# First feed-forward of a two-layer backbone: tiles 2 and 3 of the gated products by seven quarter products in place of eight

## The chip, the cores and the metric

One core of one Trainium2 chip runs the whole program. The metric is the device time in microseconds (us) of one execution, as the median of several runs. A profile is one further execution, with its own time.

## The reference, cut to what matters

Two layers work on 512 latent tokens and 256 context tokens of width 1024. Layer 0 is windowed attention, layer 1 is retention; each is followed by a gated feed-forward. The change touches the feed-forward of layer 0, where latent and context tokens go through the same weights:

```python
def swiglu(h, w_in, w_out):
    gate, up = jnp.split(h @ w_in, 2, axis=-1)
    return (jax.nn.silu(gate) * up) @ w_out

x = x + mx[5] * swiglu(modulate(rms_norm(x, norm2_g[i]), mx[3], mx[4]), ffn_w_in[i], ffn_w_out[i])
y_ctx = y_ctx + mc[5] * swiglu(modulate(rms_norm(y_ctx, norm2_g[i]), mc[3], mc[4]), ffn_w_in[i], ffn_w_out[i])
```

The inner width is 2816, or 22 tiles of 128. Beside this, all 48 modulation columns of layer 1 (`c_act @ ada_w[1] + ada_b[1]`, 6 parts of 8 columns) are worked out during this stage.

## The kernel before, in words

Everything is float32 in the reference; the kernel splits each operand of a product into a high part and a low rest (a cast on ACT, a subtraction on DVE: `split`, L157, lines L165 and L166; or `next_w`, L132, lines L140 and L141) and adds three matmuls (high by high, low by high, high by low; `mm3` at L148 to L150, `product` at L829 with its matmul at L835).

**The stage.** The hidden operand of the first feed-forward is held transposed, eight contraction pieces `A[k, half]` by two halves of 384 tokens (the 768 tokens of both streams together). The 22 inner tiles are counted by `f` from 0 and grouped 2, 4, 4, 4, 4, 4. For each tile the gate and the up product are made, then silu and the product of both, which is split into `act`. After the first tile of a group, `output` (L1007) multiplies the tiles of the group before by the second weight and adds into the residuals with `gated_add` (L253). Below, "output 0" is that of tiles 0 and 1, "output 1" that of tiles 2 to 5, and so on.

**Two ways for a tile.** `plain` (L922) makes four products of 384 columns (gate and up by two halves), each with eight contraction pieces: 8 quarter products of 12 matmuls, 96 in all. `seven` (L954) makes the same 2 by 2 block product by seven quarter products, 84 matmuls. For that it needs sums of weight quarters, four subtractions on DVE of 512 columns (L960, L962, L963, L966), then three split pairs of 1024 columns (`b11`, `b24`, `b3`) and one of 512 (`t1`, tiles `bhi` and `blo`), and on the side of the tokens the sums `S[1]` to `S[4]`. `token_sums` (L882) makes `S[1]` to `S[3]` and parks the fourth difference in the tile `crow` (L890); `last_sum` (L895) splits that into `S[4]`. After the products, seven DVE operations of 384 columns put the tile together (L977, L985, L987, and L908 and L166 twice). The seven products run in this order: 11 by `b11`, 12 by `b11`, `S[2]` by `b24`, `S[1]` by `t1`, `S[3]` by `b3`, `S[4]` by `b3`, 22 by `b24`.

Tiles 0 and 1 are made in `first_two` (L930) beside the shaping of the context half. Before, tiles 2 and 3 are plain and tiles 4 to 21 go by seven (`PLAIN = 4`).

**Buffers.** Raw weights come by SP's queue into `wraw`: two buffers in `rp`, one in `fp` (`raw_turn`, L943, one in three). Split weights have two buffers in `rp` and one in `fp`, taken in turns of three by `w_parts` (L122 and after). The operand tiles `aq` have 20 buffers: eight for `A[k, 1]`, and twelve into which the weights of two modulation units of layer 0 are loaded (units 10 and 11, L1036 to L1043); `S[1]` to `S[3]` take these twelve when the units' matmuls have read them, and `S[4]` takes those of `A[0, 1]` to `A[3, 1]`, when the last plain tile has read them. A unit ends by a transposition and two small additions (`ends`, L308 to L318); its rows wait in one of the two buffers `sq`.

**The modulation of layer 1.** `cond_rows` (L255) loads the broadcast conditioning rows into `crow` by SP's queue and applies silu; from then on `ada_next` (L947) is called at fixed places of the program: in each `seven` (behind its last split of weights), after each `seven` but the first of a group (after tile 6 all the same), and four times in each `output` but the last. Each call takes the next column from a list of 48: POOL's queue loads 512 KB into the only buffer `adaw` (L268), and DVE reduces it against the rows (L271), twice for the first 16 columns (both streams), once for the other 32, which use the free half of `crow` as a second buffer in turns.

**What sets the order.** In this stage no order is written out by hand. The instructions are put in order for each engine when the program is built, by a planner that takes program order as priority and a model of durations; on the chip each engine runs its list in that order, so an instruction that waits holds back all behind it on its engine.

Of the kernel before, what the change touches and what calls it, by code (L numbers as in the profile page):

```python
# [49 lines left out]
def dit_kernel(ctx, tc, xT, cT, crow, small, consts, masks, tabs0, tabs1, jtab, adaQ, adaN, adaT, wst, out):  # L50
# [11 lines left out]
    def T(pool, cols, tag, bufs, dt=F32):  # L62
        return pool.tile([P, cols], dt, tag=tag, bufs=bufs, name=tag)
# [42 lines left out]
    def silu(out_, in_):  # L106
        ins = nc.scalar.activation(out_, in_, AF.Silu)
        after(ins, turn["silu"][:1] or turn["lnexp"])
        turn["silu"].append(ins)
# [10 lines left out]
    def w_raw(pool=None, bufs=2):  # L120
        raw = T(pool or rp, 1024, "wraw", bufs)
        nc.sync.dma_start(raw, wst[wpos[0]])  # L122
        wpos[0] += 1
        return raw

    def w_parts(pool, own=2):

        bufs = own
        if ring:
            pool, bufs = ring[wsel[0] % len(ring)], 2  # L130
        elif wsel[0] % (2 + own) < 2:
            pool, bufs = rp, 2  # L132
        wsel[0] += 1
        return T(pool, 1024, "whi", bufs, F32R), T(pool, 1024, "wlo", bufs, F32R)

    def next_w(pool, own=2, raw=None):

        raw = raw or w_raw()
        hi, lo = w_parts(pool, own)
        nc.scalar.copy(hi, raw)  # L140
        nc.vector.tensor_tensor(lo, raw, hi, op=sub)  # L141
        return hi, lo
# [112 lines left out]
    def cond_rows(pool):  # L255

        cr = T(pool, 2048, "crow", 1)
        nc.sync.dma_start(cr, crow.broadcast_to([P, 2048]))
        for i in range(2):
            silu(cr[:, i * 1024:(i + 1) * 1024], cr[:, i * 1024:(i + 1) * 1024])  # L260
        return cr
# [537 lines left out]
    cres = load_stream(1)  # L799
    At.close()  # L800
    AK.close()
    PLAIN = 4
    WIDE = SX + SC
    THIRDS = (slice(0, 384), slice(384, WIDE))
    E = ExitStack()
# [46 lines left out]
    fp = F.enter_context(tc.tile_pool(name="fp", bufs=1, reuse_waits="tile"))  # L852
# [42 lines left out]
    def last_sum():  # L895
        for k in range(4):
            S[4, k] = parts(quarter())
            split(park[:, k * 384:(k + 1) * 384], *S[4, k])
# [5 lines left out]
    def new_act():  # L904
        return T(ep, 2 * WIDE, "act", 5, F32R)

    def finish_half(a, i, t, up):
        nc.vector.tensor_tensor(t, t, up, op=mult)  # L908
        c = THIRDS[i]
        return split(t, a[:, c], a[:, c.start + WIDE:c.stop + WIDE])  # L910

    def project_half(w, i, tag):
        o = bank(tag)
        project(w, [A[k, i] for k in range(KT)], o)
        return o

    def gate_half(w, i):
        t = t_hn(384)
        silu(t, project_half(w, i, "X"))
        return t  # L920

    def plain(w, ts=()):  # L922

        a = new_act()
        ts = [*ts, *(gate_half(w[0], i) for i in range(len(ts), 2))]
        for i in range(2):
            finish_half(a, i, ts[i], project_half(w[1], i, "Y"))
        return a

    def first_two(w, w1):  # L930

        a, ts = new_act(), []
        for i in range(2):
            X, Y = bank("X"), bank("Y")
            project_pair(w, [A[k, i] for k in range(KT)], (X, Y), None if i else context_shape)
            t = t_sq(384)
            silu(t, X)
            finish_half(a, i, t, Y)
            if i == 0:
                ts.append(gate_half(w1[0], 0))  # L940
        return a, plain(w1, ts)

    def raw_turn():  # L943
        raws[0] += 1
        return w_raw(None if raws[0] % 3 else fp, 2 if raws[0] % 3 else 1)

    def ada_next(behind):  # L947

        if ada_q:

            w = cr[:, 1024:2048] if len(ada_q) < 32 and len(ada_q) % 2 else None
            ada_tile(*ada_q.pop(0), cr, [behind], fp, w)

    def seven():  # L954
        g, u = raw_turn(), raw_turn()
        l_, r_ = slice(0, 512), slice(512, 1024)
        b11 = w_parts(fp, 1)
        split(g, *b11)
        t1 = T(fp, 512, "bhi", 1, F32R), T(fp, 512, "blo", 1, F32R)
        nc.vector.tensor_tensor(g[:, l_], u[:, l_], g[:, l_], op=sub)  # L960
        split(g[:, l_], *t1)
        nc.vector.tensor_tensor(g[:, l_], u[:, r_], g[:, l_], op=sub)  # L962
        nc.vector.tensor_tensor(g[:, r_], g[:, r_], g[:, l_], op=sub)  # L963
        b24 = w_parts(fp, 1)
        half = split(g, *b24)
        nc.vector.tensor_tensor(u[:, l_], u[:, r_], u[:, l_], op=sub)  # L966
        b3 = w_parts(fp, 1)
        split(u, *b3)
        if cr:
            ada_next(half)  # L970
        X, Y, Z = bank("X"), bank("Y"), bank("Z")
        c11, c12, c22, c21 = t_hn(384), t_hn(384), t_sq(384), t_sq(384)
        a = new_act()
        product(Y, operand["11"], b11, 0, True)
        nc.scalar.copy(c11, Y)  # L975
        product(X, operand["12"], b11, 512, True)
        nc.vector.tensor_tensor(c11, c11, X, op=add)  # L977
        silu(c11, c11)
        product(Y, operand[2], b24, 0, False)
        nc.scalar.copy(c12, Y)  # L980
        product(Z, operand[1], t1, 0, True)
        nc.scalar.copy(c21, Z)
        product(Y, operand[3], b3, 0, False)
        nc.scalar.copy(c22, Y)
        nc.vector.tensor_tensor(c22, c22, c21, op=add)  # L985
        product(Z, operand[4], b3, 512, False)
        nc.vector.tensor_tensor(c12, c12, Z, op=add)  # L987
        finish_half(a, 0, c11, c12)
        product(Y, operand["22"], b24, 512, False)
        silu(c21, Y)  # L990
        return a, finish_half(a, 1, c21, c22)
# [9 lines left out]
    def spare_w():  # L1001

        raw, w = w_raw(), (T(fp, 1024, "wraw", 1, F32R), T(fp, 1024, "adaw", 1, F32R))
        split(raw, *w)
        return w
# [30 lines left out]
    def unit(u):  # L1036
        w = [T(hq, 768, "aq", 20)[:, 0:512] for _ in range(KT - 4 * (u == 11))]
        if u == 11:
            more = T(fp, 2048, "crow", 1)
            w += [more[:, i * 512:(i + 1) * 512] for i in range(4)]  # L1040
        for k in range(KT):
            nc.sync.dma_start(w[k], adaN[u, k // 2][:, k % 2 * 512:k % 2 * 512 + 512])
        return ada_unit(u, w, pj, columns)  # L1043
# [7 lines left out]
    first = first_two([next_w(fp, 1), next_w(fp, 1)], [next_w(fp, 1), spare_w()])  # L1051
    columns = cond_columns(hq)
    ends = [unit(10), unit(11)]
    token_sums()
    f, prev = 0, None
    for gsz in FFN_GROUPS:
        acts = []
        for i in range(gsz):
            if f < PLAIN:
                acts.append(first[f] if f < 2 else plain([next_w(fp, 1, raw_turn()) for _ in range(2)]))  # L1060
                if f in (1, 2):
                    ends.pop(0)()
            else:
                if f == PLAIN:
                    last_sum()
                a, end = seven()
                acts.append(a)
                if f == PLAIN:
                    cr = cond_rows(fp)
                if i or f == PLAIN + 2:  # L1070
                    ada_next(end)
            if i == 0 and prev is not None:
                output(prev, False)
            f += 1
        prev = acts
# [464 lines left out]
    fp = F.enter_context(tc.tile_pool(name="fp", bufs=1, reuse_waits="tile"))  # L1540
# [87 lines left out]
    first = first_two()  # L1628
    f, prev = 0, None
    for gsz in FFN_GROUPS:  # L1630
        acts = []
# [158 lines left out]
```

## Time and profile before

| | us |
|---|---|
| median of 3 runs (lowest, highest) | 1782.94 (1782.34, 1787.02) |
| the profiled execution's own time | 1781.98 |
| its span in the trace | 1780.2 |
| matmuls on PE, share of the span | 97% |
| DVE, share of the span | 76% |

The profiled execution took 1.78 us more than its span, and 0.96 us less than the median of the runs. The span is cut by engine: PE is TensorE's matmuls, PEld its weight loads, DVE the vector engine, ACT the scalar engine, POOL the general engine, SP the queue that issues most transfers. A matmul's record (about 335 ns for 384 columns) is longer than its distance to the next one, since matmuls overlap; a stage is therefore measured from the start of its first matmul to the start of the next stage's. The stages around the change, by those starts in the trace:

| stage | from | to | us |
|---|---|---|---|
| tile 2, plain | 423.73 | 440.46 | 16.73 |
| output 0 | 440.46 | 457.37 | 16.91 |
| tile 3, plain | 457.37 | 474.02 | 16.65 |
| tiles 4, 5, 6, by seven | 474.02 | 517.72 | 43.70 |
| output 1 | 517.72 | 551.17 | 33.45 |
| tiles 7 to 10, by seven | 551.17 | 613.26 | 62.09 |

### The profile page before, as it was taken

Reading aid. Unit: us, or ns where it says so; the run is one execution under the profiler, and the core shown is the slowest. Engines: PE = TensorE matmul, PEld = TensorE weight load, DVE = VectorE, ACT = ScalarE, POOL = GpSimd, SP = SyncE. Lnnn points to the kernel's source line nnn. Section 1 sums busy time; section 2 is a strip of 40 time slices with the busy share of each in tenths; the row PEclk is TensorE's granted clock in tenths of the full one; section 3 lists DMA queues with packets and bytes.
Section 4 is the critical chain, followed back from the end, with each engine's and each line's share of the span. In section 5 each row is a group of like instructions: output and inputs, shape, how many; then the busy total and the mean of one; then the engine's idle time right before and its main releaser. Section 6 shows DMA issues by size and latency. Waiting matters only on the chain.

```text
span 1780.2 us, 27618 instructions
## 1 busy us (share of the span) xinstructions
PE 1721.0 (97%) x10876; PEld 1530.2 (86%) x10876; DVE 1346.5 (76%) x2347; ACT 834.1 (47%) x1465; POOL 134.4 (8%) x275
## 2 busy tenths in 40 slices
PE   6999999999999999999998999999999999999999
PEld 4777776789999999999977788898897899999998
DVE  6697786786688877787789858758758798777774
ACT  5476676454333424242455534534524564445442
POOL 0035334000000000000010000000000000000000
PEclk9999999999999999999999999999999999999999
DMA  9510002534153434353332534434433323333222
GB/s 342 229 36 25 25 1 84 161 108 139 67 154 119 154 119 153 107 157 104 119 130 86 167 107 131 148 103 137 150 104 119 95 72 111 98 112 107 95 84 83
DMA packets 59890, 206.68 MB, mean 116 GB/s; under 512 B 6640, under 2 KB 7024, under 8 KB 59504
## 3 DMA queue, kind: packets, MB, share of 16 engines
q1 hardware_dynamic: 52848, 179.75, 31.3%
q0 software_dynamic: 6912, 25.17, 4.6%
q8 instruction: 85, 1.39, 0.3%
q14 instruction: 45, 0.37, 0.1%
HBM read 202.80 MB, written 2.10 MB: 115 GB/s over the span
## 4 chain that ended last, share of the span: by engine, by line
PE 72%; DVE 15%; DMA 5%; ACT 3%; issue 2%; POOL 2%; SPq 0%; DVEq 0%; ACTq 0%; POOLq 0%
PE Y L835 13%; PE Z L835 6%; PE pj L148 6%; PE pj L150 6%; PE pj L149 6%; DMA wraw<-in_wst_dram 3%; PE X L835 3%; PE Z L1192 3%; PE Y L1179 3%; DVE wlo L166 3%; PE pT L707 2%; PE S L684 2%; PE pO L719 2%; PE X L1179 1%; POOL pr L698 1%
## 5 line engine op out<-in xcount | busy, mean ns | idle before, releaser
L165 ACT CAST whi<-wraw 128x1024 fp32r<-128x1024 f32 x171 | 179.1, 1051 | 289.9 <-PE Z L150 73.6
L166 DVE TENSOR_TENSOR wlo<-wraw,whi 128x1024 fp32r<-128x1024 f32 x171 | 208.7, 1223 | 45.4 <-ACT whi L165 45.0
L835 PE MATMUL Y<-aq,whi 128*128 128x384 f32 x576 | 156.1, 335 | 0.8 <-ACT hn L975 0.5
L141 DVE TENSOR_TENSOR wlo<-wraw,whi 128x1024 fp32r<-128x1024 f32 x84 | 102.9, 1225 | 42.0 <-ACT whi L140 41.3
L140 ACT CAST whi<-wraw 128x1024 fp32r<-128x1024 f32 x84 | 88.1, 1050 | 92.5 <-DMA wraw<-in_wst_dram 30.4
L253 DVE SCALAR_TENSOR_TENSOR res<-pj,mod,res 128x512 f32<-128x512 f32 (+1 forms) x112 | 81.6, 730 | 64.2 <-PE pj L150 63.2
L835 PEld LDWEIGHTS Y<-aq,whi 128*128 128x128 f32 x576 | 104.9, 188 | 1.7 <-ACT hn L975 0.9
L835 PE MATMUL Y<-aq,wlo 128*128 128x384 f32 x288 | 96.6, 335 | 1.5 <-DVE wlo L166 1.5
L101 ACT ACTIVATE pr<-pr,stat,qs 128x513 f32<-128x513 f32 (+2 forms) x96 | 74.2, 776 | 30.7 <-DVE stat L691 29.9
L1192 PE MATMUL Z<-whi,sA 128*128 128x512 f32 x256 | 82.2, 397 | 1.6 <-ACT whi L165 1.6
L698 POOL TENSOR_SCALAR pr<-pr,stat 128x512 f32<-128x512 f32 (+2 forms) x96 | 68.0, 721 | 86.9 <-DVE stat L695 66.7
L271 DVE CUSTOM_DVE_ANT_0 y<-adaw,crow,small_sb 128x1024 bf16<-128x1024 f32 x48 | 61.5, 1280 | 14.8 <-DMA adaw<-in_adaT_dram 14.8
L148 PE MATMUL pj<-ax,whi 128*128 128x512 f32 x176 | 68.8, 391 | 1.1 <-DVE res L253 1.1
L150 PE MATMUL pj<-ax,whi 128*128 128x512 f32 x176 | 68.7, 391 | 0.0
L149 PE MATMUL pj<-ax,wlo 128*128 128x512 f32 x176 | 68.6, 390 | 0.0
L707 PE MATMUL pT<-const_sb,pr 128*128 128x128 f32 x352 | 57.9, 284 | 10.8 <-POOL pr L698 8.5
L148 PE MATMUL pj<-act,whi 128*128 128x512 f32 x168 | 66.1, 394 | 0.0
L149 PE MATMUL pj<-act,wlo 128*128 128x512 f32 x168 | 66.0, 393 | 0.0
L150 PE MATMUL pj<-act,whi 128*128 128x512 f32 x168 | 65.6, 390 | 0.0
L707 PEld LDWEIGHTS pT<-const_sb,pr 128*128 128x128 f32 x352 | 38.8, 141 | 31.1 <-POOL pr L698 18.9
L685 DVE CUSTOM_DVE_ANT_0 pr<-S,mask,qs 128x256 f32<-128x256 f32 (+1 forms) x96 | 53.2, 568 | 14.2 <-PE S L684 7.8
L835 PE MATMUL Y<-sA,whi 128*128 128x256 f32 x304 | 60.6, 282 | 0.0
(520 smaller groups left out, 5306.2 us busy)
## 6 DMA issues: line engine op xcount, KB each, us to landing
wraw<-in_wst_dram SPq DMA_DIRECT2D x238, 512.0 KB, 3.6
adaw<-in_adaT_dram POOLq DMA_DIRECT2D x32, 512.0 KB, 3.9
wx<-in_wst_dram SPq DMA_DIRECT2D x24, 512.0 KB, 4.8
adan<-in_adaQ_dram SPq DMA_DIRECT2D x16, 512.0 KB, 8.1
adan<-in_adaN_dram SPq DMA_DIRECT2D x16, 512.0 KB, 8.8
crow<-in_adaT_dram POOLq DMA_DIRECT2D x16, 512.0 KB, 4.4
res<-in_xT_dram SPq DMA_DIRECT2D x16, 256.0 KB, 5.3
adaw<-in_adaT_dram SPq DMA_DIRECT2D x8, 512.0 KB, 4.0
```

Source lines behind the costliest of these rows:

```text
L140: nc.scalar.copy(hi, raw)
L141: nc.vector.tensor_tensor(lo, raw, hi, op=sub)
L148: nc.tensor.matmul(o, whi, xhi, start=first, stop=False)
L149: nc.tensor.matmul(o, wlo, xhi, start=False, stop=False)
L150: return nc.tensor.matmul(o, whi, xlo, start=False, stop=last)
L165: nc.scalar.copy(hi, t)
L166: return nc.vector.tensor_tensor(lo, t, hi, op=sub)
L253: return nc.vector.scalar_tensor_tensor(res[d], o, mods[l, s][:, part, d:d + 1], res[d], mult, add)
L698: nc.gpsimd.tensor_scalar(pt[:, :n], pt[:, :n], st[:, 6 + e:7 + e], 1.0, op0=mult, op1=mult)
L707: nc.tensor.transpose(tp[:, a * P:(a + 1) * P], self.pr[(0, 2, 1, 3)[a]][:, ki * P:(ki + 1) * P], ident)
L835: nc.tensor.matmul(o, p, r, start=first and k + i == 0, stop=k == 3 and i == 2, skip_group_check=not first)
L1192: ins = nc.tensor.matmul(o, p, r, start=first and k + i == 0, stop=k == 3 and i == 2, skip_group_check=not first)
```

## The change

Tiles 2 and 3 go by `seven` as the others do. With that, `last_sum` comes ahead of tile 2 (it stood ahead of tile 4), `cond_rows` comes after tile 2 (it stood after tile 4), unit 11's end comes right after tile 2's products, and the calls of `ada_next` begin with output 0 (four there, then two for each of tiles 3, 4 and 5); the list of 48 columns stays as it is and runs empty six calls earlier.

```diff
-    PLAIN = 4
+    PLAIN = 2
...
             if f < PLAIN:
-                acts.append(first[f] if f < 2 else plain([next_w(fp, 1, raw_turn()) for _ in range(2)]))
-                if f in (1, 2):
+                acts.append(first[f])
+                if f == 1:
                     ends.pop(0)()
             else:
                 if f == PLAIN:
                     last_sum()
                 a, end = seven()
                 acts.append(a)
                 if f == PLAIN:
+                    ends.pop(0)()
                     cr = cond_rows(fp)
                 if i or f == PLAIN + 2:
                     ada_next(end)
```

## The prediction

> **What bounds the kernel now.** I read the page first (sections 1, 4 and 6), then a table of windows cut at the first matmul of each stage, then the waits and the timelines inside those windows.
>
> ```profile
> span 1780.2 us, 27618 instructions
> ...
> PE 1721.0 (97%) x10876; PEld 1530.2 (86%) x10876; DVE 1346.5 (76%) x2347; ACT 834.1 (47%) x1465; POOL 134.4 (8%) x275
> ...
> PE 72%; DVE 15%; DMA 5%; ACT 3%; issue 2%; POOL 2%; SPq 0%; DVEq 0%; ACTq 0%; POOLq 0%
> ...
> adaw<-in_adaT_dram POOLq DMA_DIRECT2D x32, 512.0 KB, 3.9
> ```
>
> PE carries 72% of the chain that ended last, but DVE and DMA hold 20% of it. So a matmul less is a gain only where PE does not already wait. The windows say where that is:
>
> ```profile
> core 0: us, PE busy (x) PEld busy (x) DVE busy (x) ACT busy (x) POOL busy (x), PEclk, DMA share, GB/s
> 423.73:440.46 16.73, 16.73 (x98) 16.70 (x98) 9.46 (x19) 6.48 (x13) 0.00 (x0) 1.00 0.28 86
> 440.46:457.37 16.91, 16.91 (x98) 14.86 (x97) 12.07 (x21) 2.51 (x3) 0.00 (x0) 1.00 0.21 63
> 457.37:474.02 16.65, 16.65 (x99) 16.65 (x98) 9.54 (x15) 5.77 (x10) 0.00 (x0) 1.00 0.11 32
> 474.02:488.58 14.56, 14.56 (x86) 14.56 (x86) 9.81 (x14) 8.74 (x13) 0.00 (x0) 1.00 0.31 109
> 517.72:551.17 33.45, 33.45 (x193) 29.53 (x193) 28.01 (x47) 6.19 (x8) 2.64 (x5) 1.00 0.40 124
> 551.17:566.28 15.11, 14.83 (x86) 14.51 (x85) 12.46 (x19) 5.70 (x9) 1.06 (x2) 1.00 0.38 117
> 566.28:581.70 15.42, 14.88 (x85) 14.54 (x85) 14.52 (x24) 7.52 (x13) 0.53 (x1) 1.00 0.39 130
> 581.70:597.40 15.70, 14.84 (x85) 14.52 (x85) 15.37 (x23) 7.21 (x12) 1.05 (x2) 1.00 0.45 134
> 597.40:613.26 15.86, 15.24 (x87) 14.67 (x87) 12.19 (x20) 6.81 (x11) 1.05 (x2) 1.00 0.55 167
> 613.26:646.48 33.22, 33.22 (x192) 29.33 (x192) 24.79 (x41) 6.19 (x8) 2.64 (x5) 1.00 0.44 143
> 661.05:675.61 14.56, 14.56 (x85) 14.56 (x85) 12.89 (x20) 7.33 (x12) 1.05 (x2) 1.00 0.45 146
> ```
>
> Rows 1 and 3 are the plain tiles 2 and 3. PE and its weight loads fill them, the granted clock is 1.00, and DVE is busy for 57%: they are bound by PE. Row 4 is tile 4 by seven: 84 matmuls in 14.56 us, 0.1733 us each. Rows 6 to 9 are tiles 7 to 10, the same 84 matmuls: they take 0.55, 0.86, 1.14 and 1.30 us longer, and DVE rises to 15.37 of 15.70. What stops PE there:
>
> ```profile
> PE Y L835 <- DVE wlo L166: 1.5, 2, 0.9
> ...
> DVE y L271 <- DMA adaw<-in_adaT_dram: 7.3, 4, 3.7
> ```
>
> These rows are from the waits inside 551.17 to 613.26. PE waits for split weights, and DVE, which splits them, has stood 7.3 us at a reduction of the modulation columns whose 512 KB had not landed; all behind it in DVE's list stands too. The chip is already late here, not on arithmetic of PE, but on a single buffer. Tile 12 (661.05, 14.56 us) carries one-stream reductions only, and PE does not wait.
>
> **The change part by part.**
>
> *Matmuls.* Two tiles lose 12 matmuls each: 24 x 0.1733 = **4.16 us** less, all on the path, since rows 1 and 3 are full. The Trainium skill (TensorE: Matmul & The Clock Gate, "Back-to-back issue gap") gives N / 2.4 + 2.5 ns, 162.5 ns at 384 columns, and by that the two tiles would save 3.90 us; the row's 173.3 ns decides.
>
> *DVE's work in a tile by seven.* These groups are of the window of tile 9, with name, shape, count, busy time and mean:
>
> ```profile
> L271 DVE CUSTOM_DVE_ANT_0 y<-adaw,crow,small_sb 128x1024 bf16<-128x1024 f32 x4 | 5.1, 1282 | 0.2 <-DMA adaw<-in_adaT_dram 0.2
> L166 DVE TENSOR_TENSOR wlo<-wraw,whi 128x1024 fp32r<-128x1024 f32 x3 | 3.7, 1222 | 0.0
> L960 DVE TENSOR_TENSOR wraw<-wraw 128x512 f32<-128x512 f32 x1 | 0.7, 692 | 0.0
> L166 DVE TENSOR_TENSOR blo<-wraw,bhi 128x512 fp32r<-128x512 f32 x1 | 0.7, 691 | 0.0
> L977 DVE TENSOR_TENSOR hn<-hn,X 128x384 f32<-128x384 f32 x1 | 0.6, 553 | 0.0
> ```
>
> Weights: 3.7 + 5 x 0.69 (four sums, one low part) = 7.1 us, where a plain tile has 2 x 1.22 = 2.4; that is 4.7 more per new tile. Assembly: 7 x 0.55 = 3.9. With two two-stream columns (5.1) a tile needs 7.1 + 3.9 + 5.1 = 16.1 us of DVE against 14.56 of PE. With one-stream columns it is 13.6, and fits.
>
> *Start of tile 2.* Its operands S are split at a moment that the change doesn't move:
>
> ```profile
> 420.50 2.17 ACT L165 CAST aq<-act 128x384 fp32r<-128x384 f32 x5 [8.22 <-PE pj L308]
> ...
> 415.95 0.56 DVE L908 TENSOR_TENSOR hn<-hn,Y 128x384 f32<-128x384 f32 x1 [2.25 <-PE Y L150]
> 420.19 0.55 DVE L908 TENSOR_TENSOR hn<-hn,Y 128x384 f32<-128x384 f32 x1 [3.68 <-PE Y L150]
> ...
> 428.09 1.49 DVE L166 TENSOR_TENSOR aq<-act,aq 128x384 fp32r<-128x384 f32 x3
> ```
>
> The twelve casts cannot begin before the units' matmuls free the buffers (420.5), and the last low part ends at 429.58. Tile 2 begins at 423.73 with two products that need no S (2 x 12 x 0.1733 = 4.16), so it wants `S[2]` from 427.89, its last piece from about 429.5: just in time. `S[4]` is wanted at 423.73 + 5 x 2.08 = 434.1; its four splits (4 x 0.55) follow 429.6 and end near 432. The 4.7 us of extra weight work find 2.25 + 3.68 = 5.9 us of idle DVE ahead of 420. I put **0.5 us** here. Nothing less, as tile 2's first product has no earlier bound to lift; at most 3, if ACT's list sets the casts of `b24` behind the twelve casts (ACT busy to 425.9, then a cast of 1.05 and a low part of 1.22, while DVE is held until 429.58).
>
> *The columns move forward.* Now the rows come after tile 4:
>
> ```profile
> 473.58 0.33 SPq L258 DMA_DIRECT2D crow<-in_crow_dram  x1
> ...
> 481.06 1.06 ACT L107 ACTIVATE crow<-crow 128x1024 f32<-128x1024 f32 x1
> ...
> 491.91 1.28 DVE L271 CUSTOM_DVE_ANT_0 y<-adaw,crow,small_sb 128x1024 bf16<-128x1024 f32 x1
> ...
> 526.03 0.53 POOL L268 DMA_DIRECT2D adaw<-in_adaT_dram  x1 [7.15 <-DVE mod L271]
> 533.39 0.53 POOL L268 DMA_DIRECT2D adaw<-in_adaT_dram  x1 [6.84 <-DVE mod L271]
> ```
>
> The load follows the last `S[4]` split at once. After the change that is near 432, the second silu ends some 8.5 us later (481.06 + 1.06 less 473.58), and the first reduction comes behind output 0's second addition, about 442.5. On SP's queue only the next raw weights stand behind this load, and they wait for buffers anyway. One round of the single buffer is 533.39 - 526.03 = 7.4 us: a load of 3.9 from the page, two reductions, other work between. So 16 two-stream columns take about 118 us, from 442 to 560, and lie on output 0, tiles 3 to 6, output 1 and the start of tile 7; before, they lay on tiles 5 to 10. (The Trainium skill, DMA: Bandwidth & Descriptors, "Anatomy of one DMA", has 2.0 us + bytes / 436 GB/s, so 3.2 us as an estimate for 512 KB; with the row's 3.9 the round is longer, and the row decides.)
>
> *What goes:* the excess of tiles 7 to 10, 0.55 + 0.86 + 1.14 + 1.30 = 3.85, less 0.23 which output 2 had done ahead (33.22 for 33.45) = **3.6 us**. About two two-stream columns are left for tile 7, so I keep 0.5 of it. What is late next there is nothing: tile 12 shows it.
>
> *What comes:* Output 0 had 12.07 us of DVE in 16.91. It gets 4.7 of tile 3's weights and two or three columns (5.1 to 7.7): 22 to 24, an overrun of 5 to 7. Against it stand tile 2's idle DVE (about 2.5: 14.56 less 5.9 for the S splits in it, 2.2 for `S[4]`, 3.9 of assembly) and the parts of tile 3's weights that are wanted 4 to 8 us into it (1.2 + 1.2 + 0.7): 5.6. I take **1.5 us** of PE waiting; between none and 12.7 (four rounds of 7.4 in place of 16.91). Tiles 3 to 6 then are what tiles 7 to 10 were, four in a row with two columns each: **3.6 us**, by that nearest row; between 1 (the columns spread more evenly) and 5.2 (all four as tile 10, 1.30).
>
> *The end of unit 11* now follows tile 2's products, and its rows hold one of two `sq` buffers until then, so the tile's last assembly (five operations, 2.8 us) slips past 440. Output 1 uses it 70 us later; nothing else waits. I cost it at nothing; if output 0's context products had to wait for their bank, it would be 0.5.
>
> *Sum:* -4.16 - 3.6 + 0.5 (tile 7) + 0.5 + 1.5 + 3.6 = **-1.7 us**. Against the profiled execution's own 1781.98 that is 1780.3; on the scale of the median (0.96 above it) 1781.2. I give 1781. The ends: -4.16 - 3.6 + 1 = -6.8, and -4.16 - 3.1 + 3 + 12.7 + 5.2 = +13.6.
>
> **The rivals.**
>
> *B, both gains stay.* Tiles 3 to 6 hold `b11` in `fp` and `b24`, `b3` in `rp`; tiles 7 to 10 now hold `b24` in `fp`, which comes free only at a tile's end. In turns of three the change shifts this by two. Then `b24` can be split from product 6 of the tile before, 2.08 us earlier than now, and the waits of 0.55 to 1.30 vanish. For it: the wait named is one for `wlo`. Against it: DVE's 16.1 of 14.56 stays. Price: -4.16 - 3.6 + 0.5 + 1 = -6.3, so 1776.6.
>
> *C, slower.* DVE's list puts three or four columns into output 0, each behind its load: four rounds are 29.6 us where PE needs 16.91, 12.7 late, 2.5 of it covered. Then PE stands in output 0 and at tile 3 for about 10; tiles 3 to 6 carry fewer columns and lose 3. Price: -4.16 - 3.6 + 0.5 + 10 + 3 = +5.7, so 1788.7. It decides from the third column ahead of `b24` of tile 3. For it: output 0 has 2.1 us per addition pair and four calls, output 1 has twice that; DVE's 7.3 us at DMA. Against it: the planner orders by when it holds a load to have landed. By the Trainium skill (Perfetto Trace Analysis, "Identifying the Most-Contended Engine") the engine with the highest occupancy is the bound, and for TensorE the weight loads count. In tile 9 that is DVE with 15.37 against PEld's 14.52 of 15.70, so a stretch made like it would gain nothing from fewer matmuls; tiles 2 and 3 before, with PEld at 16.65 of 16.65, agree with the other side of the rule.
>
> *D, tile 2 starts late,* by 3 in place of 0.5, as bounded above: -1.7 + 2.5 = +0.8, so 1783.7.
>
> **How the numbers follow.** Forecast A 0.55, B 0.16, C 0.16, D 0.13. A measurement here can tell about 0.3% (5.3 us) from no change. A and D lie within that; B is faster, C slower, and 0.01 of D, with a bad output 0 as well, is slower. So faster 0.16, same 0.67, slower 0.17. The range reaches to B and nearly to C: 1776.5 to 1788. A's own range is 1778 to 1785.
>
> **What would show it.** Tiles 2 and 3 of 14.56 us plus their waits; tiles 7 to 10 back near 14.56; the waits for `wlo` and DVE's waits for `adaw` inside tiles 3 to 6; the first reduction near 442. Wrong would be: PE waiting over 3 us in output 0 (C) or ahead of product 3 of tile 2 (D), tiles 3 to 6 at 14.6 each (B), or tiles 7 to 10 still late.

## The result and the profile after

| | before | after |
|---|---|---|
| median of the runs (lowest, highest) | 1782.97 us (1782.34, 1787.02) | 1792.29 us (1788.31, 1795.85) |
| profiled execution, its span | 1781.98, 1780.2 | 1795.85, 1794.1 |

The time after by the time before is 1.0041, with a 95% interval of 1.0027 to 1.0056: **slower** by 5 to 10 us, where 1781 us was forecast and no difference that can be told. The range ended at 1788.0. The profiled execution after is the slowest of its seven, and the one before is faster than all of its seven, so the spans differ by more than the medians do (13.9 us for 9.3).

The page of the kernel after, its lines for the span, the engines, the shares of the chain, and the column's load:

```profile
span 1794.1 us, 27599 instructions
...
PE 1728.8 (96%) x10852; PEld 1535.8 (86%) x10852; DVE 1357.8 (76%) x2365; ACT 841.7 (47%) x1477; POOL 134.9 (8%) x275
...
PE 73%; DVE 12%; DMA 6%; ACT 4%; issue 2%; POOL 2%; SPq 0%; ACTq 0%; DVEq 0%; POOLq 0%
...
adaw<-in_adaT_dram POOLq DMA_DIRECT2D x32, 512.0 KB, 4.3
```

24 matmuls are gone, and yet PE is busy for 7.8 us longer. The shares of the whole span hardly moved; they don't show where the time went. The windows of the kernel after, cut at the stages' first matmuls, do. (The matmul order is mixed here: the last product of tile 2 and the first of tile 3 stand among the matmuls of output 0, so rows 1 and 2 are cut where the sixth product of tile 2 ends.)

```profile
core 0: us, PE busy (x) PEld busy (x) DVE busy (x) ACT busy (x) POOL busy (x), PEclk, DMA share, GB/s
428.08:440.87 12.79, 12.79 (x75) 12.54 (x75) 7.59 (x17) 6.98 (x15) 0.00 (x0) 1.00 0.48 176
440.87:463.57 22.70, 21.73 (x122) 18.84 (x121) 20.33 (x36) 4.91 (x8) 1.06 (x2) 1.00 0.23 69
463.57:533.54 69.97, 61.92 (x328) 58.62 (x328) 57.42 (x88) 28.05 (x45) 4.23 (x8) 0.95 0.42 129
533.54:566.42 32.88, 32.88 (x190) 29.01 (x190) 28.13 (x45) 6.18 (x8) 2.11 (x4) 1.00 0.39 127
566.42:580.98 14.56, 14.56 (x86) 14.56 (x85) 13.05 (x23) 6.55 (x10) 1.59 (x3) 1.00 0.44 143
580.98:595.54 14.56, 14.56 (x85) 14.56 (x85) 12.90 (x20) 7.33 (x12) 1.06 (x2) 1.00 0.51 150
595.54:610.10 14.56, 14.56 (x85) 14.56 (x85) 12.86 (x20) 7.33 (x12) 1.06 (x2) 1.00 0.46 145
610.10:624.67 14.57, 14.57 (x85) 14.57 (x85) 9.49 (x15) 6.81 (x11) 1.06 (x2) 1.00 0.61 182
624.67:658.12 33.45, 33.45 (x193) 29.51 (x193) 22.96 (x35) 5.62 (x7) 1.59 (x3) 1.00 0.37 110
```

Tile 2 now begins at 428.08 in place of 423.73. These 4.35 us arise far ahead of the change, at instructions that are the same in both kernels; the last section says how. So all that follows counts from tile 2's first matmul. The **stage** is the time from there to the first matmul of tile 11: 646.48 - 423.73 = 222.75 us before, 658.12 - 428.08 = 230.04 after, **+7.3 us**, about all of the 0.41%. Matched matmul by matmul, the kernel after is 10.9 us behind where output 1 ends, and tiles 7 to 10, all at 14.56 now, give 3.8 back, of which output 2 takes 0.2 again.

Row 3 is where the time is lost. Four tiles of 14.56 us, less tile 3's first product (12 x 0.1733), with some 0.6 us of output 1 are 56.8 us of matmuls, and they take 69.97: **13.2 us** too long. PE is idle for 8.0 us of it (69.97 - 61.92); the other 5 are matmuls that took longer, those first behind a stop, and those at a lower clock (0.95 on average over the row). Row 2 holds some 21.1 us of matmuls (output 0 as before, and the two products) in 22.70, **1.6** too long. What PE waits for in both rows, and DVE and ACT in the same stretch:

```profile
PE Y L835 <- ACT whi L165: 4.1, 3, 2.7
PE Y L835 <- ACT hn L975: 1.5, 1, 1.5
PE Z L835 <- ACT sq L982: 1.3, 1, 1.3
PE Y L835 <- DVE wlo L166: 1.1, 2, 0.7
```

```profile
DVE y L271 <- DMA adaw<-in_adaT_dram: 12.0, 8, 5.1
DVE hn L987 <- PE pj L315: 5.4, 1, 5.4
```

PE waits for weights (`whi`, `wlo`) that ACT and DVE split. DVE has meanwhile stood for 12.0 us, eight times, at reductions whose column had not landed, where it stood 7.3 us in the tiles 7 to 10 of before. (The longest of the eight, 5.1 us up to 531.22, comes behind PE's last stop, at 522.72; PE is busy throughout after it.) The second row lies in tile 2: DVE stands 5.4 us ahead of an addition that reads product 6 (`Z`; the profile puts it down to the matmul behind that product). That was the cushion that the prediction counted on. It is no loss in itself: every kernel below with tiles 2 and 3 by seven has it, the fastest too. ACT's list, and then DVE's in the same stretch:

```profile
447.30 0.51 ACT L165 CAST act<-sq 128x384 fp32r<-128x384 f32 x1
463.77 0.48 ACT L975 COPY hn<-Y 128x384 f32<-128x384 f32 x1 [15.96 <-PE Y L835]
465.89 1.05 ACT L165 CAST whi<-wraw 128x1024 fp32r<-128x1024 f32 x1 [1.64 <-PE X L835]
467.89 1.99 ACT L165 CAST whi<-wraw 128x1024 fp32r<-128x1024 f32 x2 [0.95 <-DVE wraw L963]
```

```profile
464.36 1.28 DVE L271 CUSTOM_DVE_ANT_0 y<-adaw,crow,small_sb 128x1024 bf16<-128x1024 f32 x1 [0.85 <-DMA adaw<-in_adaT_dram]
465.97 1.28 DVE L271 CUSTOM_DVE_ANT_0 y<-adaw,crow,small_sb 128x1024 bf16<-128x1024 f32 x1
467.17 0.69 DVE L963 TENSOR_TENSOR wraw<-wraw 128x512 f32<-128x512 f32 x1
```

The copy of tile 3's first product waits 15.96 us, because that product's matmuls are spread through output 0; the casts of tile 3's remaining weights stand behind it. But the copy is over at 464.25, and what ends the casts' wait is L963, the sum from which `b24` is made. It stands in DVE's list behind both reductions of the third column, which wait 0.85 us for their load. So when tile 3 starts in earnest its weights aren't there, and PE stops for them twice (0.75 and 0.68 us). PE's largest stop, 2.65 us up to 519.85, has the same chain: the cast that it waits for, at 518.75, needs an L963 at 517.90, which stands on DVE behind reductions at 513.01 and 514.69, the first of them 1.96 us late at its load. The columns come in rounds of the single buffer, 7 to 10 us each:

```profile
506.31 0.53 POOL L268 DMA_DIRECT2D adaw<-in_adaT_dram  x1 [7.43 <-DVE mod L271]
516.27 0.53 POOL L268 DMA_DIRECT2D adaw<-in_adaT_dram  x1 [9.43 <-DVE mod L271]
524.16 0.53 POOL L268 DMA_DIRECT2D adaw<-in_adaT_dram  x1 [7.37 <-DVE mod L271]
534.49 0.53 POOL L268 DMA_DIRECT2D adaw<-in_adaT_dram  x1 [9.79 <-DVE mod L271]
```

### The profile page after: what moved, and what is told of

Same layout as the page of the kernel before. It is cut to its first block, busy times and chain, and to the rows that moved or that the text cites. A ratio compares the mean times of both kernels' runs of the same rounds, so it can differ in the third digit from the quotient of the medians.

```text
span 1794.1 us, 27599 instructions
## 1 busy us (share of the span) xinstructions
PE 1728.8 (96%) x10852; PEld 1535.8 (86%) x10852; DVE 1357.8 (76%) x2365; ACT 841.7 (47%) x1477; POOL 134.9 (8%) x275
## 4 chain that ended last, share of the span: by engine, by line
PE 73%; DVE 12%; DMA 6%; ACT 4%; issue 2%; POOL 2%; SPq 0%; ACTq 0%; DVEq 0%; POOLq 0%
PE Y L835 13%; PE Z L835 6%; PE pj L148 6%; PE pj L150 6%; PE pj L149 6%; PE Y L1180 4%; PE Z L1193 4%; PE X L835 3%; DMA wraw<-in_wst_dram 2%; DVE wlo L166 2%; PE pj L1193 2%; PE pT L707 2%; DMA adaw<-in_adaT_dram 2%; PE pO L719 2%; PE S L684 2%
## 5 line engine op out<-in xcount | busy, mean ns | idle before, releaser
L835 PE MATMUL Y<-aq,whi 128*128 128x384 f32 x640 | 175.6, 338 | 6.1 <-ACT whi L165 4.1
L835 PEld LDWEIGHTS Y<-aq,whi 128*128 128x128 f32 x640 | 117.6, 189 | 8.2 <-ACT whi L165 5.1
L835 PE MATMUL Y<-aq,wlo 128*128 128x384 f32 x320 | 108.0, 338 | 1.1 <-DVE wlo L166 1.1
L101 ACT ACTIVATE pr<-pr,stat,qs 128x513 f32<-128x513 f32 (+2 forms) x96 | 74.2, 775 | 31.7 <-DVE stat L691 30.9
L835 PEld LDWEIGHTS Y<-aq,wlo 128*128 128x128 f32 x320 | 60.6, 189 | 1.8 <-DVE wlo L166 1.8
```

The source lines that it names most:

```text
L101: ins = nc.scalar.activation(*args, **kw)
L835: nc.tensor.matmul(o, p, r, start=first and k + i == 0, stop=k == 3 and i == 2, skip_group_check=not first)
```

## The experiments

The theory: the loss is the modulation columns, which now fall on output 0 and tiles 3 to 6, eleven calls by output 1. The first rivals: that tiles 2 and 3 cost it themselves, by their weight work on DVE, their buffers or the matmul order; and, among the columns, that it is the loads, or DVE's arithmetic, or only the calls in output 0 (rival C). "To output 1" is what a kernel lies behind the kernel before at the end of output 1, counted from tile 2. Ratios are to runs of the kernel before on the same chip; each changed kernel ran two to twelve times (two: after, no columns). The last two columns are read from one profiled execution each. Every kernel's order is planned anew, so its lists can differ in more than the edit.

| kernel | ratio (95%) | to output 1 | stage |
|---|---|---|---|
| before | 1 | 0 | 222.75 |
| after | 1.0041 (1.0027 to 1.0056) | +10.9 | 230.0 |
| late columns | 0.9980 (0.9965 to 0.9994) | -1.9 | 221.2 |
| after, no columns | 0.9949 (0.9929 to 0.9969) | -3.8 | 215.3 |
| before, no columns | 0.9974 (0.9963 to 0.9984) | 0.0 | 219.1 |
| matmuls in program order | 1.0018 (1.0005 to 1.0031) | +6.4 | 225.5 |
| columns without loads | 0.9979 (0.9968 to 0.9989) | +1.4 | 220.5 |
| three calls in output 0 | 1.0010 (0.9995 to 1.0025) | +6.2 | 225.3 |
| two calls in output 0 | 0.9996 (0.9981 to 1.0010) | +2.4 | 221.6 |
| one call in output 0 | 0.9975 (0.9964 to 0.9986) | -1.8 | 217.3 |
| one call in each of tiles 3 to 5 | 0.9971 (0.9958 to 0.9984) | -1.5 | 217.6 |
| both of these | 0.9943 (0.9928 to 0.9958) | -3.8 | 217.0 |
| thinned out further | 0.9966 (0.9953 to 0.9980) | -3.6 | 215.8 |
| before, thinned out | 0.9983 (0.9971 to 0.9995) | 0.0 | 220.3 |

In every row but one the ratio's interval holds what the stage alone would give. "Both of these" is 0.57% faster, where its stage gives 0.32%; the runs don't show where the rest comes from.

**Is it the columns?** In the kernel after, the rows are loaded after tile 4 again, as before; the calls begin where they began before:

```diff
                 if f == PLAIN:
                     ends.pop(0)()
+                if f == 4:
                     cr = cond_rows(fp)
-                if i or f == PLAIN + 2:
+                if cr and (i or f == 6):
                     ada_next(end)
```

> Tiles 2 and 3 by seven as in the changed kernel, but the conditioning rows are loaded after tile 4 and the columns of layer 1 are called where they were before the change. The stage is measured from the first matmul of tile 2 to the first of tile 11: 222.75 us before, 230.04 after. Theory 1 (the columns, brought forward onto output 0 and tiles 3 to 6, overload DVE and hold it at the single buffer): PE does not wait in tiles 2 to 6, tiles 7 to 10 wait 3.6 again, stage 218.6 (217.8 to 220), time about 4 us under before. Theory 2 (the two tiles by seven are themselves late, by their weights, their sums or the turn of three buffers shifted by two, wherever the columns lie): stage 226 or more, time 3 to 8 us over before.

221.2, nearer to the columns' 218.6 than to 226, though 2.6 above it. The columns are back on tiles 5 to 10, and at the end of output 1 the kernel is 1.9 us ahead where it was 10.9 behind. It isn't 4.2 ahead there, since PE stops once, 1.62 us for a copy on ACT (`hn`, at 507.43), and tiles 7 to 10 wait as they did before.

**And without them?** In both kernels, loads and reductions go and layer 1's modulation is a constant:

```diff
-            w = cr[:, 1024:2048] if len(ada_q) < 32 and len(ada_q) % 2 else None
-            ada_tile(*ada_q.pop(0), cr, [behind], fp, w)
+            ada_q.pop(0)
...
+    for s in range(2):
+        nc.gpsimd.memset(mods[1, s], 0.5)
```

> The changed kernel without the 48 columns of layer 1: their loads and their reductions are left out and the modulation of layer 1 is a constant. Theory 1: no waits of PE in tiles 2 to 10, stage 215 (214.5 to 216). Theory 2: the waits stay in tiles 3 to 6, 222 or more.

> The kernel before, with the same left out. Both theories: stage 222.75 - 3.6 = 219.1, as the columns are what tiles 7 to 10 wait for; so that the two without columns differ by the matmuls alone, 4.2, by theory 1.

215.3 and 219.1: two tiles by seven in place of plain are then worth 3.8 us, close to the 4.16 worked out, and no wait of PE is left. So tiles 2 and 3, their weights and their buffers cost nothing in themselves, and all of the 14.7 us between -3.8 and +10.9 come with the columns.

**Is it the order of the matmuls?** The first matmul of each product, and of each group in an output, is held behind the last one of the product or group before, so PE's list stands in program order:

```diff
+                if k + i == 0:
+                    after(ins, pe_last)
+        pe_last[:] = [ins]
...
-        nc.tensor.matmul(o, whi, xhi, start=first, stop=False)
+        after(nc.tensor.matmul(o, whi, xhi, start=first, stop=False), behind)
```

> The changed kernel with PE's list in program order over the stage: the first matmul of each product and of each output is put behind the last of the one before, so that tile 3's first product no longer lies in pieces among output 0's matmuls, and tiles 3 to 6 no longer lie in one another. The stage (first matmul of tile 2 to first of tile 11) is 222.75 before and 230.04 after. If the mixed order is what costs: 225 or less. If DVE's load and its waits set the pace whatever PE's order: 228 to 232.

225.5, between the two. Of the 14.7 us, 4.5 go with the mixed order and 10.2 stay. How the order makes them isn't shown. It isn't ACT's long wait for the copy of tile 3's first product alone: with matmuls in program order the copy waits 16.84 us, as that product now comes behind all of output 0, and a kernel below where it waits 15.16 us (one call in each of tiles 3 to 5) is faster than before.

**Is it the loads?** The reductions stay, on resident rows scaled by 0.001 (so layer 1's modulation is not the reference's); no column is loaded:

```diff
-        (nc.gpsimd if l else nc.sync).dma_start(w, adaT[l, j])
+        if not l:
+            nc.sync.dma_start(w, adaT[l, j])
...
-            w = cr[:, 1024:2048] if len(ada_q) < 32 and len(ada_q) % 2 else None
+            w = cr[:, 0:1024]
```

> The changed kernel with all 48 reductions of layer 1's columns at their places, but none of their loads: each reduces the conditioning rows already on chip, scaled by 0.001, so the modulation of layer 1 is another. If the single buffer and its loads are what holds DVE (12 us of standing in the stage): PE's waits of 15 us fall to 2 to 6, stage 217 to 221. If DVE's sum of work is enough (16.1 us in a tile of 14.56): 226 or more.

+1.4 to output 1: 9.5 of the 14.7 us need the loads, 5.2 come from DVE's arithmetic and order alone. What the loads do is two things that this run doesn't part. DVE stands at them, and beside them the raw weights land later: from tile 2 to the end of output 1 a median of 4.3 us from issue to landing in the kernel after, 3.6 without the loads, and DVE stood 1.8 us at one of them (508.97).

**Which calls?** Only the calls in output 0 are cut from four to one, or only those in tiles 3 to 5 from two to one each, or both:

```diff
-            if cr and not final and s == 0 and d % 2:
+            if cr and not final and s == 0 and (d % 2 if f > 2 else d == 7):
...
-        if cr:
+        if cr and f > 5:
             ada_next(half)
```

> The changed kernel with one call for a column in output 0 in place of four; tiles 3 to 5 keep two each. Rival C of the prediction (the columns in output 0 hold the weights of tile 3): the stage falls by 8 or more, to 222 or less. Forecast A with a larger size (four tiles in a row with two columns each): it falls by 2 to 4 only, 226 to 228, as the list of columns is worked off two in a tile all the same.

> The changed kernel with one call for a column in each of tiles 3, 4 and 5 in place of two; output 0 keeps its four. Forecast A with a larger size: the stage falls by 5 to 8, to 222 to 225. Rival C: by 2 at most, 228 to 230.

> The changed kernel with the six surplus calls for a column taken out at the front: one call in output 0 (in place of four) and one for each of tiles 3, 4 and 5 (in place of two). Theory 1: nine columns less by tile 6 become six less, so PE's waits of 15 us in the stage fall to about half, stage 221 to 225. Theory 2: 229 to 231.

All three lost less than was expected: the first came out as rival C had it, the second below both, the third below its 221 to 225. Either cut of three calls takes away 12.4 to 12.7 of the 14.7 us, and the two together 14.7. So it isn't a place that decides, neither output 0 (rival C) nor the tiles, but the number of calls by output 1. With four calls in output 0 and one in each of tiles 3 to 5, all that is left of PE's stops over 0.3 us are the two for tile 3's `b24` (0.68 and 0.69 us). I then held that it was a threshold, with the whole loss as soon as the calls come faster than the round; the next two, with three calls in output 0 and with two, tell that from a like share for each call:

```diff
-            if cr and not final and s == 0 and d % 2:
+            if cr and not final and s == 0 and d % 2 and (f > 2 or d > 1):
...
+            if cr and not final and s == 0 and d % 2 and (f > 2 or d > 3):
```

> The kernel after with three calls for columns in output 0 in place of four, all else as after: ten calls by output 1 in place of eleven. From the first matmul of tile 2 to the end of output 1 the kernel after took 10.9 us more than before, and with one call in output 0 1.8 us less than before. Theory that each call costs a like share: about 4.2 us of it go, so 6.7 more than before. Threshold theory: the calls of tiles 3 to 6 still come faster than the round of the buffer, so 9 to 11 more.

> The kernel after with two calls for columns in output 0 in place of four, all else as after: nine calls by output 1 in place of eleven. From the first matmul of tile 2 to the end of output 1 the kernel after took 10.9 us more than before, and with one call in output 0 1.8 us less. Theory that each call costs a like share: 2.4 more than before. Threshold theory: still 4 to 8 more, and the rest goes with the next call.

+6.2 and +2.4: a like share, and my threshold falls. The stretch from 12.8 us into tile 2 to output 1's first low-part matmul holds nearly the same matmuls in all of these. One row each, by ten, nine, eight and five calls (the kernel after, with eleven, has rows 2 and 3 above: 92.67 us, DVE busy 77.75):

```profile
438.29:526.17 87.88, 83.00 (x450) 77.64 (x449) 73.53 (x117) 32.05 (x53) 4.75 (x9) 0.96 0.36 114
```

```profile
438.44:522.28 83.84, 79.99 (x448) 76.75 (x446) 73.41 (x118) 32.46 (x52) 4.25 (x8) 0.98 0.35 114
```

```profile
438.24:517.85 79.61, 78.08 (x448) 75.22 (x446) 71.07 (x113) 32.83 (x54) 3.70 (x7) 1.00 0.37 113
```

```profile
437.20:514.83 77.63, 77.63 (x448) 75.35 (x446) 66.44 (x104) 32.88 (x53) 2.65 (x5) 1.00 0.30 96
```

Length and DVE are the first and the fourth figure. 92.67, 87.88, 83.84, 79.61: each call less saves 4.0 to 4.8 us. Then 77.63 for three calls less: 0.7 each, and PE is full. That looks like an engine from which more is asked than the stretch has time for: from about eight calls on, each further one lengthens the stretch by its own price, below that it is nearly free. The price of 4.2 us on average is more than the two reductions (2 x 1.28); the rest goes with standing at loads and with what PE's stops cost besides (below). DVE's waits for `adaw` in the stretch, again by ten, nine, eight and five calls:

```profile
DVE y L271 <- DMA adaw<-in_adaT_dram: 9.8, 6, 4.7
```

```profile
DVE y L271 <- DMA adaw<-in_adaT_dram: 8.6, 5, 3.9
```

```profile
DVE y L271 <- DMA adaw<-in_adaT_dram: 3.1, 4, 1.2
```

```profile
DVE y L271 <- DMA adaw<-in_adaT_dram: 3.0, 1, 3.0
```

DVE's busy time and this standing fill 89.8 of the 92.67 us, then 83.3 of 87.88, 82.0 of 83.84, 74.2 of 79.61 and 69.4 of 77.63. The sum isn't the loss, as the longest standing by eleven, ten and nine calls (5.1, 4.7 and 3.9 us) lies behind PE's last stop; the price of a call is read from the lengths.

**How far does it go?** First the kernel after, with one call in output 0, six in each other output, and the calls inside the tiles in tiles 11 to 18 only; then the kernel before, thinned out likewise:

```diff
-            if cr and not final and s == 0 and d % 2:
+            if cr and not final and s == 0 and (d < 6 if f > 2 else d == 7):
...
-        if cr:
+        if cr and 11 <= f <= 18:
```

```diff
-            if cr and not final and s == 0 and d % 2:
+            if cr and not final and s == 0 and d < (6 if f < 11 else 5):
...
-        if cr:
+        if cr and f > 10:
```

> The kernel after, with the columns thinned out as far as the list allows: one call in output 0, six in each of outputs 1 to 4, and the calls inside the tiles only in tiles 11 to 18. The stage from tile 2 to tile 11 took 222.75 us before, 230.04 after, 217.0 with one call in output 0 and one in each of tiles 3 to 5, and 215.3 without any columns. Threshold theory (all of the loss is columns that come faster than the round of the single buffer): close to the floor without columns, 215.3 to 216.3, so some 6.5 to 7.4 less than before, and 0.3 to 0.4% faster. Rival (each call costs its own share, wherever it stands): the calls moved into outputs 1 and 2 bring the cost back there, and the stage stays at 217 or above.

> The kernel before, tiles 2 and 3 still plain, with its columns thinned out in the same way: outputs 0 and 1 without a change in what they can call, six calls in an output before tile 11 and five behind, and the calls inside the tiles only from tile 11 on. Threshold theory: the excess of tiles 7 to 10 (3.6 us) goes and nothing comes in its place, so the stage from tile 2 to tile 11 is 219.1 to 219.8 (222.75 before), the time 0.1 to 0.2% lower than before; the difference to the thinned kernel after is then the matmuls alone, 3.8 to 4.2 us. Rival: the spacing alone gives all that the thinned kernel after gained, 216 or below.

215.8, near the floor of 215.3, and 220.3, half a microsecond above what was expected. Their difference of 4.5 us is again about the 4.16 of the matmuls. The two kernels after with the most calls moved back (both of these, thinned out further) beat both kernels of the change: 0.9943 and 0.9966. Their intervals overlap, and the stages stand the other way round (217.0 and 215.8), so the runs don't say which is the better one. A second buffer for the columns was not tried.

## Why the prediction was wrong, step by step

- **Matmuls, -4.16: right.** 3.8 (without columns) and 4.5 (thinned out). Tiles 8 and 9 after, 84 matmuls in 14.56, keep the pitch of 0.1733 us, 24 of which make 4.16; the 3.90 us that follow, as an estimate, from the formula of the Trainium skill for the gap of an isolated matmul (TensorE: Matmul & The Clock Gate, "Back-to-back issue gap") lie within these runs' spread as well, but its 162.5 ns isn't the pitch of a row here.
- **Tiles 7 to 10, -3.6: right** to the tenth. The 0.5 kept for tile 7 is 0, although the last two-stream column lies in it, as forecast (573.1 and 574.9).
- **Start of tile 2, 0.5: right**, rival D is out. Row 1 after has tile 2's first six products in 12.79 us, with PE full.
- **First reduction near 442: over 2 us late.** 449.18 less the 4.35 is 444.8.
- **Output 0, 1.5 of PE waiting: right in its size (1.6), wrong in what it left behind.** The size is in part luck: of its two waits one, 0.53 us, is for an addition that stands behind a column on DVE, and the other, 0.44, for a copy on ACT (`sq`). The overrun of 5 to 7 us was set against 5.6 us of cover. Of that, DVE's idle time in tile 2 was not to be had: it stood 5.4 us at an addition of tile 2 with nothing else ready, as tile 3's `b11` waits for the buffer in `fp` that is free only at product 6. And the weights that "are wanted 4 to 8 us into" tile 3 stood, by L963, behind the third column's reductions on DVE. The overrun didn't vanish; it went on into tile 3.
- **The step that failed: "Tiles 3 to 6 then are what tiles 7 to 10 were", 3.6, with an upper end of 5.2. It measured 13.2.** The mechanism was the one named (split weights late, because DVE stands at columns in a single buffer), but an excess was carried over from one stretch to another as if it belonged to the tiles. It belongs to a balance: DVE's work and its standing on one side, PE's matmuls on the other, over the whole stretch until the debt is paid. For output 0 and tiles 3 to 6 such a balance stood in the prediction's own figures: 22 to 24 + 4 x 16.1 = 86 to 88 us of DVE against 16.91 + 4 x 14.56 = 75.2 of PE, 11 to 13 late. That this comes near the 14.8 measured (1.6 + 13.2) is in part luck: 4.7 us of tile 3's weights stand in both of its terms, and it has no term for standing. In the trace DVE is busy for 77.75 us where PE needs 77.6, and stands at loads for 12.0 more, of which the last 5.1 come behind PE's last stop. Tiles 7 to 10 before had output 1 ahead of them, 28.01 us of DVE in 33.45, and their own DVE came to 54.5 us, and 7.3 of standing, in 62.09: that only just fits. With output 0 relieved of three calls, tiles 3 to 6, all their columns kept, lose no more than 2.0 us. The ends that the prediction gave its sum, -6.8 and +13.6 us, hold the +9.3 measured; the range was drawn narrower.
- **Unit 11's end, nothing: right** as far as it goes; DVE's 5.4 us at the matmul of that end appear with fewer calls too, in the fastest kernel among others.
- **The rivals.** B is out, since tiles 3 to 6 take far more than 14.56 each. C had the sign, and nearly the size (+5.7; the stage measured +7.3), but not its place (PE stops in tiles 3 to 6, hardly in output 0). Its condition came true, a third column ahead of `b24` of tile 3, and cost two stops there (0.75 and 0.68 us) where C had about 10 with output 0; and there is no step at the third call (four, three, two and one call give +10.9, +6.2, +2.4 and -1.8). C at 0.16 was the case in which the columns in output 0 are more than what comes after can bear, and the balance above would have spoken for it.
- **What remains open:** how the 14.7 us divide among loads, DVE's arithmetic and the matmul order, and by what the order acts. Without loads 9.5 go, with program order 4.5, with three calls less 12.4 to 12.7; they overlap, as each brings the stretch nearer to the point where DVE keeps up.

## What to carry to other kernels

When a change moves side work onto another stretch, make one balance over that whole stretch: all the work and all the standing at loads of the engine that does it, against the time of the bounding engine. An excess that a similar stretch showed holds only with the same slack ahead of it, and slack counts only if the waiting engine has something in its list that it can do then. Beyond the balance each further item costs its full price (here 4.0 to 4.8 us a column); so move the side work together with the change, as the two thinned-out kernels do, rather than accept where it falls.

## What the runs showed of the hardware

**A stop of PE costs more than its length, since the clock falls after it.** The largest stop in the kernel after, in windows of 1 us; the figure ahead of the last two is the granted clock:

```profile
517.00:518.00 1.00, 0.20 (x2) 0.00 (x0) 1.00 (x4) 0.46 (x2) 0.00 (x0) 1.00 0.75 98
518.00:519.00 1.00, 0.00 (x0) 0.00 (x0) 1.00 (x3) 1.00 (x4) 0.00 (x0) 1.00 0.70 246
519.00:520.00 1.00, 0.15 (x1) 0.15 (x1) 0.98 (x3) 1.00 (x2) 0.00 (x0) 1.00 0.45 180
520.00:521.00 1.00, 0.29 (x1) 0.03 (x1) 0.77 (x1) 1.00 (x2) 0.00 (x0) 0.80 0.00 0
521.00:522.00 1.00, 0.42 (x1) 0.29 (x1) 1.00 (x3) 1.00 (x3) 0.00 (x0) 0.50 0.00 0
...
526.00:527.00 1.00, 1.00 (x4) 0.90 (x4) 0.14 (x1) 0.30 (x1) 0.00 (x0) 0.50 0.47 139
527.00:528.00 1.00, 1.00 (x7) 0.92 (x6) 0.00 (x0) 0.18 (x1) 0.00 (x0) 0.79 0.99 328
```

PE did almost nothing for 3 us, and from 520.6 to 527.4 its clock is at half (0.4 us of the fourth row and of the last), though PE is full again from 522.7: some 4.7 us of matmuls at 0.32 us each in place of 0.173, about 2.2 us lost beside the waits. It happened too where there were nine calls (a wait of 2.30, then 3.4 us at half), ten (2.16 and 1.29 close together, then nearly 7 us) and with matmuls in program order (1.47 and 2.02 close together, then 3.4 us). Where the longest wait in the stage was 1.62 us or less (all the other kernels), the clock stayed at 1.00. The Trainium skill (TensorE: Matmul & The Clock Gate, "Part 1: The HAM clock gate") has half rate after an idle window of about 3.4 us, with windows that run freely: the length of the dips agrees, 3.4 us or twice that; a whole such window of idle time was not needed here, a stop of 2.3 us was enough.

**The same dips move a profile where nothing was changed.** Two windows far ahead of the stage, after and then before, with the same code:

```profile
260.00:280.00 20.00, 19.48 (x119) 16.09 (x120) 15.50 (x52) 11.60 (x33) 6.55 (x21) 0.83 0.17 53
320.00:340.00 20.00, 16.80 (x68) 11.84 (x68) 10.09 (x20) 10.87 (x19) 1.43 (x4) 0.83 0.52 184
```

```profile
260.00:280.00 20.00, 18.76 (x135) 14.75 (x134) 16.85 (x59) 13.07 (x37) 8.31 (x22) 1.00 0.35 120
320.00:340.00 20.00, 16.81 (x75) 12.71 (x74) 12.76 (x21) 9.69 (x15) 0.93 (x2) 0.91 0.61 211
```

In that stretch PE has many small waits, and the clock falls in one execution and not in the next: a mean of 0.83 over 20 us is 6.8 us at half, 0.91 is 3.6, the same dips of 3.4 us as above, two and one of them. By tile 2 the profiled execution after was 4.35 us behind, of which 2.1 came in the first of these windows and 1.6 in the second, and 2.2 more came behind the stage, where the clock fell more often too. Together that is nearly as much as the effect under study: a stage is to be measured from its own first matmul, and the whole by many runs.
